# Three adaLN halves move from TensorE to VectorE, one of them into the S5-input stage, and the weight stream gets six buffers instead of seven

## The chip, the cores and the metric

One core of one Trainium2 chip. The metric is the device time of one launch, in microseconds, as the median of several runs; the profiled execution is one more launch, with its own time.

## What is computed

One conditioned decoder block on 256 tokens of width 2048, all in fp32. The condition vector `c` gives six vectors by one product with a 2048 x 12288 matrix (adaLN): shift, scale and gate for the mixer and for the MLP.

```
ada = (cond @ w_ada + b_ada)
sh1, sc1, gt1, sh2, sc2, gt2 = split(ada, 6)
u = rmsnorm(h, g_mix) * (1 + sc1) + sh1
q, kc, vc, ks_, vs_, kw, vw, g_nsa, u_ssm, g_merge = split(u @ w_in, ...)
y_a = nsa_attention(q, kc, vc, ks_, vs_, kw, vw, g_nsa, ...)
y_s = gelu(s5_ssm(u_ssm, ...))
y_b = y_s * sigmoid(y_s @ w_glu + b_glu)
g_a, g_b = split(sigmoid(g_merge), 2)
h = h + gt1 * ((g_a * y_a + g_b * y_b) @ w_out)
u2 = rmsnorm(h, g_mlp) * (1 + sc2) + sh2
h = h + gt2 * (square(relu(u2 @ w_up)) @ w_down)
return rmsnorm(h, g_final)
```

`sh1` and `sc1` are needed at once. `gt1`, `sh2`, `sc2` are needed behind the output projection, and `gt2` at the end: these are the later adaLN vectors.

## The kernel before

All weights flow through one stream of units. A unit loads one raw tile of 128 x 1024 fp32 values (512 KB) with one DMA on SyncE's queue (L210) into a ring of `RAW` = 7 buffers; the load of unit i+7 is issued at the start of turn i (i+5 while the generator `outs` is at work). A weight unit is split for an exact product: ScalarE copies it to `hi` in a shorter type (the helper at L117), VectorE computes `lo` = raw − hi (L120), and TensorE runs three matmuls for each 128 x 128 block, hi by hi, hi by lo and lo by hi (L315, L317, L318), two units behind the copy. An adaLN unit is not split: it takes the raw tile as it lies.

The list `units` is written in order of the stages: `sh1`/`sc1` with the first columns of `w_in`, the compressed keys and values (`vs`, 16 value tiles, and `compress`), the stage called E, gate A (`ga`), queries (`q`), gate B (`gb`), `glu`, `out`, `up`, `down`. E holds the last six value tiles and the tile of the attention gates; beside them the generator `in` makes the S5 inputs in 16 steps, each with 16 small matmuls (L809) and four ScalarE copies of 128 x 256 from PSUM. Generators like it (the S5 scan in gate A, q and the start of gate B, its outputs later in gate B, attention beside `glu`) are moved on by the count of weight units; adaLN units don't count.

The later vectors come in halves of 1024 columns, 16 raw tiles each. Six of them (`gt1`, `sh2`, `sc2`) are put between the weight units of E, gate A, q, gate B, `glu` and `out`; the table `ADA2` says how many tiles each of these stages takes, in this order, and `ADA_PE` which halves go over TensorE. There are two forms:

- on TensorE (`ada2_pe_units`): a pair of raw tiles is contracted with `cond` in 32 small matmuls (L998), four pairs fill a quarter, then ScalarE copies, transposes (L1007) and a VectorE reduction (L1009);
- on VectorE (`ada2_units`): 16 operations on 128 x 1024 add raw tile times `cond` column into an accumulator (L129, after one at L124), then four matmuls with ones (L965), a copy, four small transposes (L974), one addition.

Before the change `ADA2` gives E none and `glu` two halves; halves 0, 1, 3, 4, 5 go over TensorE, half 2 (in gate B) over VectorE. The two halves of `gt2`, in the up stage, are on VectorE in both kernels.

`weave(main, extra, tail=6, head=0)` spreads the extra units over the main ones up to the last `tail`:

```
    want = max(0, min(len(extra), (i + 1 - head) * len(extra) // (len(main) - tail - head)))
    res += extra[ie:want]
```

E calls it with seven main units and the default tail of six, so that all extra units come right behind the first main unit. `W_GLU` is (6, 10) and `W_OUT` is (8, 0), as (tail, head). In `out` each weight unit of the first 1024 columns also prepares its block of the mixed y, with turns between VectorE and ScalarE (L129 RX, L117 RB, L129 RB).

Of the kernel before, what the change touches and what calls it, by code (L numbers as in the profile page):

```python
# [9 lines left out]
FT = mybir.dt.float32  # L10
# [13 lines left out]
    0, 2048, 3072, 3584, 4096, 4608, 5120, 5168, 7216, 9264)  # L24
A_SH1, A_SC1, A_GT1, A_SH2, A_SC2, A_GT2 = (i * D for i in range(6))

RAW, HI, LO = 7, 3, 3
SPLIT = 2
ADA2 = [0, 16, 16, 16, 32, 16]
ADA_PE = (0, 1, 3, 4, 5)  # L30
SCAN_END = 0.4
ATTN_WAIT = 5
AS0, AS1 = 2, 13
# [48 lines left out]
def block_kernel(ctx, tc, cst_in, x, c, w_ada, b_ada, g_mix, w_in, w_ck2, pe_ck,  # L82
# [8 lines left out]
    sp = ctx.enter_context(tc.tile_pool(name="staging", bufs=1))  # L91
# [3 lines left out]
    def bank(tag):  # L95
        return pp_.tile([128, 512], FT, tag=tag, name=tag)
# [4 lines left out]
    def stage():  # L101
        return sp.tile([128, 512], FT, tag="st", name="st", bufs=ST)

    def big4():
        return sp.tile([128, 1024], FT, tag="s4", name="s4", bufs=2)

    def region(tag, n):
        return rp.tile([128, n], FT, tag=tag, name=tag)
# [7 lines left out]
    def copy(out, in_, scale=1.0):  # L116
        A.activation(out=out, in_=in_, func=AF.Copy, scale=scale)  # L117

    def tt(out, a, b, op):
        V.tensor_tensor(out=out, in0=a, in1=b, op=op)  # L120

    def ts(out, a, s1, op1, s2=None, op2=None):
        if s2 is None:
            V.tensor_scalar(out=out, in0=a, scalar1=s1, scalar2=None, op0=op1)  # L124
        else:
            V.tensor_scalar(out=out, in0=a, scalar1=s1, scalar2=s2, op0=op1, op1=op2)

    def stt(out, a, s, b, op0, op1):
        V.scalar_tensor_tensor(out=out, in0=a, scalar=s, in1=b, op0=op0, op1=op1)  # L129
# [59 lines left out]
    def defer(n, fn):  # L189
        later.setdefault(now[0] + n, []).append(fn)  # L190
# [220 lines left out]
    def merge(a, b, lead=LEAD, tail=TAIL):  # L411
        res = a[:lead]
        a = a[lead:]
        ia = 0
        for ib, u in enumerate(b):
            res.append(u)
            want = min(len(a), (ib + 1) * len(a) // (len(b) - tail))
            res += a[ia:want]
            ia = want
        return res  # L420
# [45 lines left out]
    def keep_x():  # L466
        nc.gpsimd.dma_start(out=d_xT, in_=xT)
        yield
# [480 lines left out]
    def ada2_units(vec, half, tag):  # L949
        off = (A_GT1, A_SH2, A_SC2, A_GT2)[vec] + 1024 * half  # L950
        hold = {}

        def run(u, kt):
            if kt == 0:
                hold["a"] = big4()
                ts(hold["a"], u.raw, cond[:, 0:1], OP.mult)
            else:
                stt(hold["a"], u.raw, cond[:, kt:kt + 1], hold["a"], OP.mult, OP.add)
            if kt == 15:
                defer(FIN_GAP, fin1)  # L960

        def fin1():
            ps = bank(tag)
            for i in range(2):
                PE.matmul(out=ps[32 * i:32 * i + 32, :], lhsT=ones32, rhs=hold["a"][:, 512 * i:512 * i + 512],  # L965
                          start=True, stop=True, tile_position=(0, 32 * i))
            hold["s"] = stage()
            copy(hold["s"][0:64], ps[0:64, :])
            defer(FIN_GAP, fin2)

        def fin2():
            ps = bank(tag)
            for j in range(4):
                PE.transpose(ps[:, 64 * j:64 * j + 64], hold["s"][0:64, 128 * j:128 * j + 128], ident[0:64, 0:64])  # L974
            k0 = 16 * vec + 8 * half
            bk = 32 + 16 * vec + 8 * half
            tt(ada2[:, k0:k0 + 8].rearrange("p (h j) -> p h j", h=2),
               ps[:, 0:256].rearrange("p (j h n) -> p h j n", j=4, h=2)[:, :, :, 0],
               bada_c[:, bk:bk + 8].rearrange("p (h j) -> p h j", h=2), OP.add)
            if vec == 2 and half == 1:  # L980
                stt(s2, sc2_c, 1.0, gmlp_c, OP.add, OP.mult)
        return [Unit([(lambda r: r, w_ada[0, kt * 128:(kt + 1) * 128, off:off + 1024])],
                     lambda u, k=kt: run(u, k), gemm=False) for kt in range(16)]
# [523 lines left out]
    with tc.manual_schedule():  # L1507
        units += ada1_units(0)
        for ci in range(1, len(chunks)):
            units += merge(ada1_units(ci), first_pass_units(ci - 1))  # L1510
        units += first_pass_units(len(chunks) - 1)
        e2 = []
        for h in range(6):
            if h in ADA_PE:
                e2 += ada2_pe_units(h // 2, 2 * (h % 2)) + ada2_pe_units(h // 2, 2 * (h % 2) + 1)
            else:
                e2 += ada2_units(h // 2, h % 2, "T12")
        marks["vs"] = len(units)
        vs = vs_units()
        units += vs[:VA] + weave(vs[VA:VB], compress_units(), 0) + vs[VB:VC]  # L1520
        marks["E"] = len(units)
        dist = iter(np.cumsum([0] + ADA2))

        def some(a=[next(dist)]):
            lo_, a[0] = a[0], next(dist)
            return e2[lo_:a[0]]
        units += weave(vs[VC:] + gate_unit(), some())
        marks["ga"] = len(units)
        units += weave(proj_units(C_GA, d_g, 0, AF.Tanh, 0.5, True), some())
        marks["q"] = len(units)  # L1530
        units += weave(proj_units(C_Q, d_q, 0, AF.Copy, HD ** -0.5, True), some())
        marks["gb"] = len(units)
        units += weave(proj_units(C_GB, d_g, 16, AF.Tanh, 0.5, False), some(), *W_GB)
        marks["glu"] = len(units)
        units += weave(glu_units(), some(), *W_GLU)
        marks["out"] = len(units)
        units += weave(out_units(), some(), *W_OUT)
        marks["up"] = len(units)
        up = up_units()
        up[0].lo_first = up[1].lo_first = True  # L1540
        units += up[:UP_WAIT] + weave(up[UP_WAIT:], [u for h in range(2) for u in ada2_units(3, h, "T3")])
        marks["down"] = len(units)
        units += down_units()

        xs, r2 = prelude()

        def at_(name, f, nxt):
            return int(marks[name] + f * (marks[nxt] - marks[name]))
        bgs = [
            dict(name="x", gen=x_chain(xs, r2), start=0, end=6, total=6, tick=True),  # L1550
            dict(name="xw", gen=keep_x(), start=marks["vs"] - KX, end=marks["vs"] - KX, total=1),
            dict(name="ld", gen=s5_loads(), start=LD0, end=LD0, total=1, tick=True),
            dict(name="ld2", gen=s5_loads2(), start=LD1, end=LD2, total=4, tick=True),
            dict(name="p1", gen=s5_prep(), start=P10, end=PB, total=P1A, tick=True),
            dict(name="p2", gen=s5_operands(), start=PB + 1, end=marks["vs"] - P11, total=P1N + 4 * sum(CY) + IDLE + IDLE2, tick=True),
            dict(name="cmp", gen=compress_setup(), start=marks["vs"] - 2, end=marks["vs"] + 3, total=12),
            dict(name="lam", gen=s5_lambda(), start=marks["vs"] + EM0, end=marks["vs"] + EM1, total=12, tick=True),
            dict(name="keep", gen=s5_keep(), start=marks["vs"] + EM1 + 1, end=marks["E"] - 2, total=4, tick=True),
            dict(name="chan", gen=s5_channels(), start=marks["vs"] + U0, end=marks["vs"] + U1, total=4, tick=True),
            dict(name="stk", gen=s5_inputs(), start=marks["vs"] + KI, end=marks["vs"] + KI, total=1),  # L1560
            dict(name="in", gen=(x_ for _ in range(1) for x_ in un["E"]), start=marks["E"] + 1, end=marks["ga"] - 1, total=16),
            dict(name="scan", gen=s5_scan(), start=marks["ga"], end=at_("gb", SCAN_END, "glu"), total=128),
            dict(name="mat0", gen=s5_matrices(0), start=marks["q"] + CL0, end=marks["q"] + CL1, total=4, tick=True),
            dict(name="mat1", gen=s5_matrices(1), start=marks["gb"] + CM0, end=marks["gb"] + CM1, total=4, tick=True),
            dict(name="outs", gen=s5_outputs(), start=at_("gb", SCAN_END, "glu") + 1, end=marks["glu"] - 1, total=17),
            dict(name="load", gen=attn_setup(), start=marks["glu"] + AS0, end=marks["glu"] + AS1, total=13),
            dict(name="tb", gen=load_tb(), start=marks["glu"] + TB0, end=marks["glu"] + TB1, total=4, tick=True),
            dict(name="attn", gen=attention(), start=marks["glu"] + ATTN_WAIT, end=marks["out"] - 2, total=34),
        ]
        run_units(bgs)  # L1570
# [47 lines left out]
```

## Time and profile before

| | us |
|---|---|
| median of 3 runs | 1780.44 |
| lowest, highest | 1776.47, 1782.63 |
| the profiled execution, its time | 1776.92 |
| its span | 1775.1 |
| TensorE busy | 1718.9 (97%) |
| TensorE weight loads busy | 1620.6 (91%) |
| VectorE busy | 1108.5 (62%) |
| ScalarE busy | 856.3 (48%) |

The mean granted TensorE clock of the span is 0.989. The stages lie in the span like this: first stage to about 290, `vs` and `compress` to 329, E to 381, gate A and q to about 565, gate B to 701, `glu` and attention to 895, `out` to 1010, up to 1376, down to the end. TensorE's busy time is an upper measure, since its matmuls overlap; a window of the trace gives for each engine its busy time, the count of its instructions, the granted clock and the share of the DMA engines.

### The profile page before, as it was taken

The page shows a single profiled execution, that of the slowest core. Times are in us where ns is not written, and L with a number is a line of the kernel's source. Part 1 is how long each engine was busy: PE and PEld are TensorE (multiplying, and loading weights), DVE is VectorE, ACT ScalarE, POOL GpSimd, SP SyncE. Part 2 cuts the span into 40 slices and gives each one's busy share as a digit, 9 for nine tenths or more (in the row PEclk, how much of TensorE's full clock was granted, in tenths as well). Part 3 has the DMA queues.
Part 4 walks back from the last instruction along what each step waited for, and adds up shares of the span by engine and source line. Part 5 has one row for each costly group of instructions (what it writes and reads, how often), then busy time and mean ns, then how long its engine had stood idle before and what let it go on. Part 6 is the DMA issues. An engine that isn't in the chain of part 4 may idle for free.

```text
span 1775.1 us, 37647 instructions
## 1 busy us (share of the span) xinstructions
PE 1718.9 (97%) x15710; PEld 1620.6 (91%) x15710; DVE 1108.5 (62%) x2032; ACT 856.3 (48%) x1379; POOL 29.4 (2%) x51
## 2 busy tenths in 40 slices
PE   6999999999999999999999999999999999999997
PEld 4788898789999988888899999999999999999997
DVE  4868468347888966666656575555555555565554
ACT  3433443754333477655544454444444544464444
POOL 1000000300000000000000000000000000000000
PEclk8999999999999999999999999999999999999998
DMA  9988756858888867876667567777777565556662
GB/s 349 327 275 315 260 180 206 267 160 296 274 274 283 254 211 243 296 244 211 214 198 262 176 219 235 235 227 224 240 234 227 179 183 184 181 176 184 184 181 81
DMA packets 121802, 406.26 MB, mean 229 GB/s; under 512 B 13904, under 2 KB 18480, under 8 KB 120864
## 3 DMA queue, kind: packets, MB, share of 16 engines
q1 hardware_dynamic: 114480, 385.49, 67.1%
q10 hardware_dynamic: 5408, 9.75, 1.5%
q0 software_dynamic: 1744, 8.62, 1.4%
q8 instruction: 123, 2.02, 0.4%
q14 instruction: 47, 0.39, 0.1%
HBM read 384.84 MB, written 16.88 MB: 226 GB/s over the span
## 4 chain that ended last, share of the span: by engine, by line
PE 87%; DVE 5%; ACT 4%; DMA 2%; issue 1%; ACTq 0%; SPq 0%; DVEq 0%
PE A L315 25%; PE A L317 24%; PE A L318 24%; PE T L998 2%; DVE lo L120 2%; PE T L343 2%; ACT hi L117 1%; ACT RX L117 1%; DMA raw<-in_l_ada_dram 1%; PE T L809 1%; PE A L897 1%; DMA raw<-in_l_vals_dram 1%; PE A L899 1%; PE A L898 1%; PE T L737 0%
## 5 line engine op out<-in xcount | busy, mean ns | idle before, releaser
L120 DVE TENSOR_TENSOR lo<-raw,hi 128x1024 fp32r<-128x1024 f32 (+1 forms) x497 | 607.0, 1223 | 507.8 <-ACT hi L117 504.0
L117 ACT ACTIVATE hi<-raw 128x1024 fp32r<-128x1024 f32 (+1 forms) x497 | 523.1, 1055 | 580.5 <-PE A L317 539.0
L315 PE MATMUL A<-RU,hi 128*128 128x256 f32 x2560 | 740.2, 289 | 3.3 <-ACT hi L117 1.5
L318 PE MATMUL A<-RU,lo 128*128 128x256 f32 x2560 | 728.0, 284 | 1.5 <-DVE lo L120 1.5
L317 PE MATMUL A<-RU,hi 128*128 128x256 f32 x2560 | 727.8, 284 | 0.0
L315 PEld LDWEIGHTS A<-RU,hi 128*128 128x128 f32 x2560 | 494.3, 193 | 27.7 <-issue 20.9
L318 PEld LDWEIGHTS A<-RU,lo 128*128 128x128 f32 x2560 | 494.4, 193 | 2.0 <-DVE lo L120 1.9
L317 PEld LDWEIGHTS A<-RU,hi 128*128 128x128 f32 x2560 | 494.7, 193 | 0.3 <-DVE RU L129 0.2
L315 PE MATMUL A<-RB,hi 128*128 128x256 f32 x1280 | 363.9, 284 | 1.4 <-ACT RB L117 1.2
L317 PE MATMUL A<-RB,hi 128*128 128x256 f32 x1280 | 362.6, 283 | 0.2
L318 PE MATMUL A<-RB,lo 128*128 128x256 f32 x1280 | 362.2, 283 | 0.0
L315 PEld LDWEIGHTS A<-RB,hi 128*128 128x128 f32 x1280 | 245.7, 192 | 3.4 <-ACT RB L117 1.6
L317 PEld LDWEIGHTS A<-RB,hi 128*128 128x128 f32 x1280 | 245.7, 192 | 0.6 <-DVE RB L129 0.5
L318 PEld LDWEIGHTS A<-RB,lo 128*128 128x128 f32 x1280 | 245.6, 192 | 0.0
L117 ACT ACTIVATE RB<-RX 128x256 fp32r<-128x256 f32 x160 | 64.3, 403 | 27.4 <-DVE RX L129 27.4
L120 DVE TENSOR_TENSOR RX<-A,RX 128x512 f32<-128x512 f32 x60 | 40.4, 687 | 30.2 <-PE A L318 29.2
L129 DVE SCALAR_TENSOR_TENSOR s<-raw,cond,s 128x1024 f32<-128x1024 f32 x45 | 57.6, 1279 | 0.1
L117 ACT ACTIVATE RX<-T 128x256 f32<-128x256 f32 (+2 forms) x81 | 39.8, 638 | 35.8 <-PE T L1204 26.6
L120 DVE TENSOR_TENSOR RB<-RX,RB 128x256 fp32r<-128x256 f32 x128 | 53.4, 418 | 1.6 <-ACT RB L117 1.6
L343 PE MATMUL T<-raw,cond 128*32 128x256 f32 x512 | 40.8, 413 | 10.0 <-DMA raw<-in_l_ada_dram 10.0
L998 PE MATMUL T<-raw,cond 128*32 128x128 f32 x1280 | 43.2, 276 | 2.0 <-ACT RX L117 2.0
L998 PEld LDWEIGHTS T<-raw,cond 128*32 128x32 f32 x1280 | 32.5, 109 | 8.4 <-ACT RX L117 4.2
(237 smaller groups left out, 1248.1 us busy)
## 6 DMA issues: line engine op xcount, KB each, us to landing
raw<-in_l_ada_dram SPq DMA_DIRECT2D x144, 512.0 KB, 4.9
raw<-in_w_in_dram SPq DMA_DIRECT2D x144, 512.0 KB, 4.6
raw<-in_w_up_dram SPq DMA_DIRECT2D x128, 512.0 KB, 4.2
raw<-in_w_down_dram SPq DMA_DIRECT2D x128, 512.0 KB, 4.5
raw<-in_w_ada_dram SPq DMA_DIRECT2D x48, 512.0 KB, 4.1
raw<-in_w_glu_dram SPq DMA_DIRECT2D x32, 512.0 KB, 5.1
raw<-in_w_out_dram SPq DMA_DIRECT2D x32, 512.0 KB, 5.8
raw<-in_l_keys_dram SPq DMA_DIRECT2D x16, 512.0 KB, 4.4
```

The lines of the kernel that those rows point to most:

```text
L117: A.activation(out=out, in_=in_, func=AF.Copy, scale=scale)
L120: V.tensor_tensor(out=out, in0=a, in1=b, op=op)
L129: V.scalar_tensor_tensor(out=out, in0=a, scalar=s, in1=b, op0=op0, op1=op1)
L315: PE.matmul(out=o, lhsT=w.hi[:, at], rhs=xh, start=first and j % 2 == 0, stop=False, skip_group_check=True)
L317: PE.matmul(out=o, lhsT=w.hi[:, at], rhs=xl, start=False, stop=False, skip_group_check=True)
L318: PE.matmul(out=o, lhsT=w.lo[:, at], rhs=xh, start=False, stop=last, skip_group_check=True)
L343: PE.matmul(out=ps[q:q + 32, :], lhsT=cond[:, t0 + t:t0 + t + 1].to_broadcast([128, 32]), rhs=r[:, t, :], start=t0 == 0, stop=t0 == 12, ti ...
L809: PE.matmul(out=ps[h][:, (w * 2 + r_) * 128:(w * 2 + r_) * 128 + 128], lhsT=bl[c4 // 2][64 * h:64 * h + 64, (gw + w) % 16, r_, :], rhs=stk ...
L897: PE.matmul(out=o, lhsT=xh, rhs=u.hi[:, at], start=kt == 0, stop=False)
L898: PE.matmul(out=o, lhsT=xl, rhs=u.hi[:, at], start=False, stop=False)
L899: PE.matmul(out=o, lhsT=xh, rhs=lo[:, at], start=False, stop=kt == 15)
L998: PE.matmul(out=ps[q:q + 32, 0:128], lhsT=cond[:, kt:kt + 1].to_broadcast([128, 32]), rhs=r[:, kt % 8, :], start=kt < 4, stop=kt >= 12, ti ...
```

## The change

The ring of raw tiles has six buffers. `ADA2` gives each of the six stages one half. Only halves 1 (gate A) and 2 (q) go over TensorE; halves 0 (E), 3 (gate B), 4 (`glu`) and 5 (`out`) go over VectorE. The accumulators have three buffers instead of two, and the halves 4 and 5 use the PSUM bank T3 for their ending.

```diff
-RAW, HI, LO = 7, 3, 3
+RAW, HI, LO = 6, 3, 3
-ADA2 = [0, 16, 16, 16, 32, 16]
-ADA_PE = (0, 1, 3, 4, 5)
+ADA2 = [16, 16, 16, 16, 16, 16]
+ADA_PE = (1, 2)
...
-        return sp.tile([128, 1024], FT, tag="s4", name="s4", bufs=2)
+        return sp.tile([128, 1024], FT, tag="s4", name="s4", bufs=3)
...
-                e2 += ada2_units(h // 2, h % 2, "T12")
+                e2 += ada2_units(h // 2, h % 2, "T12" if h < 4 else "T3")
```

SyncE's queue around the start of E (the value tiles `l_vals`, the adaLN tiles `w_ada`, the gate tile `l_gate`, and a store of compress, `d_c`):

```order
 L210 DMA raw<-in_l_vals_dram 128x1024 x2
 L760 DMA d_c<-RX 128x1024
-L210 DMA raw<-in_l_vals_dram 128x1024 x2
+L210 DMA raw<-in_l_vals_dram 128x1024
+L210 DMA raw<-in_w_ada_dram 128x1024
 L760 DMA d_c<-RX 128x1024
-L210 DMA raw<-in_l_vals_dram 128x1024 x3
+L210 DMA raw<-in_w_ada_dram 128x1024 x15
+L210 DMA raw<-in_l_vals_dram 128x1024 x5
 L210 DMA raw<-in_l_gate_dram 128x768
```

All 16 adaLN loads now stand ahead of the last five value tiles.

VectorE beside attention, from the end of one head's scores to the next weight tile's lo, before:

```order
L1169 TENSOR_REDUCE RX<-T_9198 128x1
L1170 TENSOR_REDUCE RX<-T_9198 128x2
L124 TENSOR_SCALAR RX<-RX 128x3
L120 TENSOR_TENSOR lo<-raw,hi 128x1024
L120 TENSOR_TENSOR RX<-RX,cst 128x2x16
L1187 TENSOR_REDUCE RX<-RX 128x2
```

and of the changed kernel:

```order
L1169 TENSOR_REDUCE RX<-T_9217 128x1
L1170 TENSOR_REDUCE RX<-T_9217 128x2
L124 TENSOR_SCALAR RX<-RX 128x3
L129 SCALAR_TENSOR_TENSOR s_9099<-raw,cond,s_9099 128x1024
L120 TENSOR_TENSOR lo<-raw,hi 128x1024
L120 TENSOR_TENSOR RX<-RX,cst 128x2x16
```

One accumulation (`s`) has come in ahead of the lo; it is so once for each of 16 weight tiles.

VectorE in the first half of `out`, two weight tiles with their mixing, before:

```order
L120 TENSOR_TENSOR lo<-raw,hi 128x1024
L129 SCALAR_TENSOR_TENSOR RX<-RB_8555,RX 128x256
L129 SCALAR_TENSOR_TENSOR RB_10742<-RX,RB_10742 128x256
L120 TENSOR_TENSOR lo<-raw,hi 128x1024
L129 SCALAR_TENSOR_TENSOR RX<-RB_8555,RX 128x256
L129 SCALAR_TENSOR_TENSOR RB_10742<-RX,RB_10742 128x256
```

and of the changed kernel, three tiles:

```order
L120 TENSOR_TENSOR lo<-raw,hi 128x1024
L129 SCALAR_TENSOR_TENSOR RX<-RB_8613,RX 128x256
L129 SCALAR_TENSOR_TENSOR RB_10476<-RX,RB_10476 128x256
L129 SCALAR_TENSOR_TENSOR s_10525<-raw,cond,s_10525 128x1024
L120 TENSOR_TENSOR lo<-raw,hi 128x1024
L129 SCALAR_TENSOR_TENSOR RX<-RB_8613,RX 128x256
L129 SCALAR_TENSOR_TENSOR RB_10476<-RX,RB_10476 128x256
L120 TENSOR_TENSOR lo<-raw,hi 128x1024
```

An accumulation stands behind two of three tiles there.

## Rows read from the trace of the kernel before

**Rows 1.** The page: busy time and share of each engine, and the shares by engine of the chain that ended last.

```profile
PE 1718.9 (97%) x15710; PEld 1620.6 (91%) x15710; DVE 1108.5 (62%) x2032; ACT 856.3 (48%) x1379; POOL 29.4 (2%) x51
...
PE 87%; DVE 5%; ACT 4%; DMA 2%; issue 1%; ACTq 0%; SPq 0%; DVEq 0%
```

**Rows 2.** Windows by stage: E, gate A and q with the start of gate B, attention, `out`. Columns: the window, its length, busy time (and instructions) of TensorE, its weight loads, VectorE, ScalarE, GpSimd, the granted TensorE clock, the DMA share, GB/s.

```profile
329.00:381.00 52.00, 46.26 (x400) 38.48 (x400) 12.43 (x17) 40.66 (x79) 9.25 (x17) 1.00 0.61 190
381.00:637.00 256.00, 255.62 (x2471) 250.21 (x2472) 214.03 (x592) 98.77 (x118) 0.00 (x0) 0.99 0.81 267
...
756.00:868.00 112.00, 108.75 (x1128) 91.72 (x1127) 69.26 (x220) 59.36 (x191) 0.00 (x0) 1.00 0.66 222
868.00:1010.00 142.00, 140.03 (x1305) 132.78 (x1297) 90.04 (x168) 68.91 (x128) 0.56 (x1) 1.00 0.69 230
```

**Rows 3.** The page's costliest groups: busy time, mean ns of one, idle time before.

```profile
L129 DVE SCALAR_TENSOR_TENSOR s<-raw,cond,s 128x1024 f32<-128x1024 f32 x45 | 57.6, 1279 | 0.1
```

**Rows 4.** Timeline of TensorE in gate A (a pair of adaLN tiles and the weight tiles around it) and in gate B (the ending of the half on VectorE). Columns: start, length, engine, line, operation, count.

```profile
389.07 1.08 PE L998 MATMUL T<-raw,cond 128*32 128x128 f32 x32
390.08 0.38 PE L315 MATMUL A<-RU,hi 128*128 128x256 f32 x1
...
398.89 1.08 PE L998 MATMUL T<-raw,cond 128*32 128x128 f32 x32
...
701.65 1.05 PE L965 MATMUL T<-s,cst 128*32 128x512 f32 x4
702.63 0.39 PE L315 MATMUL A<-RU,hi 128*128 128x256 f32 x1
```

**Rows 5.** Timeline of ScalarE in E: three steps of the S5 inputs (12 copies), the hi copy of value tile 13, and the first of gate A. The last column is the idle time before, with what ended it.

```profile
335.77 5.50 ACT L117 ACTIVATE RX<-T 128x256 f32<-128x256 f32 x12 [2.99 <-DMA raw<-in_l_vals_dram]
341.06 1.06 ACT L117 ACTIVATE hi<-raw 128x1024 fp32r<-128x1024 f32 x1
...
373.19 1.06 ACT L117 ACTIVATE hi<-raw 128x1024 fp32r<-128x1024 f32 x1
```

**Rows 6.** Timeline of VectorE in E: the lo of value tile 11, then of 12 and 13.

```profile
331.07 1.23 DVE L120 TENSOR_TENSOR lo<-raw,hi 128x1024 fp32r<-128x1024 f32 x1 [2.55 <-ACT hi L117]
332.81 1.23 DVE L120 TENSOR_TENSOR lo<-raw,hi 128x1024 fp32r<-128x1024 f32 x1 [0.51 <-ACT hi L117]
342.16 1.23 DVE L120 TENSOR_TENSOR lo<-raw,hi 128x1024 fp32r<-128x1024 f32 x1 [8.13 <-ACT hi L117]
```

**Rows 7.** Windows of 5 us, columns as in Rows 2: the start of E, the start of gate A, and a stretch of the first stage.

```profile
325.00:330.00 5.00, 5.00 (x28) 4.07 (x27) 2.75 (x5) 2.31 (x4) 3.59 (x7) 1.00 1.04 343
335.00:340.00 5.00, 4.32 (x51) 3.69 (x48) 0.00 (x0) 4.23 (x10) 0.00 (x0) 1.00 1.03 411
...
380.00:385.00 5.00, 3.62 (x22) 3.57 (x23) 4.90 (x14) 1.33 (x2) 0.00 (x0) 0.78 0.61 204
...
75.00:80.00 5.00, 1.30 (x20) 0.36 (x16) 4.93 (x9) 0.00 (x0) 0.00 (x0) 0.90 1.00 361
80.00:85.00 5.00, 5.00 (x41) 4.07 (x34) 4.34 (x15) 1.06 (x1) 0.00 (x0) 0.76 1.03 411
```

**Rows 8.** The view of the adaLN tiles of the VectorE form (`w_ada`): time from issue to landing.

```profile
DMA to landing us min/median/max: 3.5/4.1/5.8
```

**Rows 9.** Timeline of TensorE at the start of gate A.

```profile
381.38 0.32 PE L922 MATMUL T<-cst,st 48*128 48x48 f32 x2 [2.52 <-ACT st L917]
381.63 0.39 PE L315 MATMUL A<-RU,hi 128*128 128x256 f32 x1
```

**Rows 10.** Timeline beside attention: TensorE at the start of two heads that lie three weight tiles apart, then VectorE through these three tiles.

```profile
760.40 0.62 PE L1153 MATMUL T<-RX 128*128 128x272 f32 x2
782.63 0.62 PE L1153 MATMUL T<-RX 128*128 128x272 f32 x2
...
776.62 0.18 DVE L120 TENSOR_TENSOR RX<-RX,cst 128x32 f32<-128x32 f32 x1
...
778.51 0.42 DVE L129 SCALAR_TENSOR_TENSOR RX<-RB,A 128x256 f32<-128x256 f32 x1
...
783.29 0.45 DVE L120 TENSOR_TENSOR T<-T,cst 128x272 f32<-128x272 f32 x1
...
789.10 0.41 DVE L129 SCALAR_TENSOR_TENSOR RX<-RB,A 128x256 f32<-128x256 f32 x1
...
792.23 0.45 DVE L120 TENSOR_TENSOR T<-T,cst 128x272 f32<-128x272 f32 x1 [0.81 <-PE T L1153]
797.70 1.23 DVE L120 TENSOR_TENSOR lo<-raw,hi 128x1024 fp32r<-128x1024 f32 x1 [2.91 <-ACT hi L117]
```

**Rows 11.** Timeline in the first half of `out`: VectorE from lo to lo, then TensorE at two pairs that lie three weight tiles apart.

```profile
917.26 1.23 DVE L120 TENSOR_TENSOR lo<-raw,hi 128x1024 fp32r<-128x1024 f32 x1 [0.52 <-ACT hi L117]
...
919.30 0.42 DVE L129 SCALAR_TENSOR_TENSOR RB<-RX,RB 128x256 fp32r<-128x256 f32 x1 [0.48 <-ACT RB L117]
920.25 1.23 DVE L120 TENSOR_TENSOR lo<-raw,hi 128x1024 fp32r<-128x1024 f32 x1 [0.52 <-ACT hi L117]
...
919.74 1.08 PE L998 MATMUL T<-raw,cond 128*32 128x128 f32 x32
929.57 1.08 PE L998 MATMUL T<-raw,cond 128*32 128x128 f32 x32
```

**Rows 12.** Waits of 20 to 330 (waiting instruction, what released it: idle us, times, longest), and the page's DMA issues (KB, median us to landing).

```profile
PE T L343 <- DMA raw<-in_l_ada_dram: 3.7, 2, 3.1
...
raw<-in_w_down_dram SPq DMA_DIRECT2D x128, 512.0 KB, 4.5
```

## Prediction

> **What bounds the kernel now.** I read three things, in this order. First the page's busy shares and the chain that ended last: TensorE works 1718.9 us of the 1775.1 us span and holds 87% of that chain [rows 1], so in the mean every TensorE microsecond removed is a microsecond gained. Second, because that mean covers stages with different limits, the windows by stage [rows 2]. The gate-A stage (381 to 637) is TensorE alone, 255.62 of 256. The stage with the S5 inputs (329 to 381, called E below) is not: TensorE 46.26 of 52, VectorE nearly idle with 12.43, ScalarE busy for 40.66. Attention (756 to 868) has TensorE at 108.75 of 112 and VectorE at 69.26; the output projection (868 to 1010) 140.03 of 142 beside 90.04. Third, in E, attention and the output projection, the rows of the engines that feed TensorE, since there the question is whether something else ends later once TensorE has less to do. "Half" below is one 1024-column piece of an adaLN vector, 16 raw tiles.
>
> **What TensorE gives up.** Three halves leave it: two beside GLU and attention, one beside the output projection; the gate-A stage and the q stage carry one each, as before. A half is 8 pairs of raw tiles; a pair stands on TensorE from 389.07 to 390.08, 1.01 us, and between two pairs lie three weight tiles: 389.07 to 398.89 is 9.82, so a weight tile costs (9.82−1.01)/3 = 2.94 [rows 4]. The half is 8.1, three are 24.2. Each of the three halves on VectorE still needs the four matmuls with ones, 701.65 to 702.63, 0.98 [rows 4]; the small transposes of the old form and of the new one I set against each other. Net −21.3, if TensorE paced every place where something goes in or out. On VectorE a half is 16 operations of 1.28 us [rows 3], 20.5 us; whether they are hidden decides everything, stage by stage.
>
> **E: +13, bounds +4 and +19.** This is the one stage that receives work without losing any. The 16 raw tiles all stand right behind the eleventh of the 16 value tiles, and ScalarE runs in program order. So the hi copy of value tile 12 stands in ScalarE's queue ahead of the 13 S5-input steps that remain (of 16; 3 run before it), each four copies, 5.50/3 = 1.83 us [rows 5]; that copy waits for its tile, whose load stands behind 16 adaLN loads in a ring of six. VectorE is free once the lo of value tile 11 is done, 331.07+1.23 = 332.3 [rows 6]. The load of value tile 12 needs the buffer of the 11th adaLN tile: 332.3 + 11×1.28 + some 1.5 for late arrivals (the DMA queues are full here, share 1.04 at 325 to 330 and 1.03 at 335 to 340 [rows 7]) = 347.9. An adaLN tile lands 4.1 us after its issue [rows 8], and value tiles come the same way: the hi copy starts near 352.
>
> From the hi copy at 341.06 (value tile 13) to the first of gate A at 373.19 the stage today takes 32.1 us for five weight tiles and 13 steps [rows 5]; from value tile 12 there are six tiles, 1.06 us of ScalarE more: 33.2. Gate A then starts at 385.2 instead of 373.19: +12. Meanwhile TensorE finishes the tiles and the steps that it has and idles some ten microseconds. What that does to the clock the trace shows twice. It granted 0.76 in 80 to 85 after TensorE had been busy for 1.30 of the 5 us before, and 0.78 in 380 to 385 [rows 7], around an idle of 2.52 us; behind that, 48 matmuls took 381.63 to 389.07, 7.44 us, instead of the 5.88 of two weight tiles [rows 9, 4]. I add 1 (the steps that follow are bound by ScalarE). The Trainium skill ("TensorE: Matmul & The Clock Gate", section "HAM oscillation — how this bites in real kernels") says that idle gaps between bursts of matmuls put the array back to its low clock, a rule that speaks against this change; the rows of the clock agree with it.
>
> Low bound: the block starts at 329 and nothing arrives late: 329 + 11×1.28 + 3.5, the shortest landing [rows 8], = 346.6; then ScalarE without a gap, 13×1.83 + 6×1.06 = 30.2, to 376.8: +3.6. High bound: the 16 tiles come at the 343 GB/s of 325 to 330 [rows 7], 24.5 us for 8.4 MB, 4.0 more than the accumulation and 2.5 more than I allowed; landing at 5.8 instead of 4.1; 2 more of clock: +19.
>
> **GLU and attention: −6.5, bounds −15 and +1.** Today three weight tiles with two heads and three pairs take 22.23 us, 760.40 to 782.63 [rows 10]. Without the pairs TensorE needs 22.23 − 3×1.01 = 19.20. In the changed order every weight tile has one accumulation on VectorE, in front of its lo. A tile's turn on VectorE is lo, head work, accumulation. For the first of two heads: 1.23, then 783.29 to 789.51 = 6.22, then 1.28: 8.73. For the second: 1.23, then 792.23 to the next lo at 797.70 = 5.47, in which the accumulation fits (the lo waits 2.91 for the hi copy, which stands behind the exponentials on ScalarE): 6.70. For the tile between: 1.23, 776.62 to 778.93 = 2.31, 1.28: 4.82 [rows 10]. The sum, 20.25, is above 19.20: VectorE, in turn with ScalarE, becomes the limit, and the gain is 2.0 of 3.0. Over 16 tiles that is −10.6 at best. Part is lost, because the ring assumes that ScalarE answers as fast as now though its inputs come later: I take −7.5, two thirds of it, and add 0.98 for the ones-matmuls. Bounds: all 16 pairs gained, −16.2 + 0.98; none, +1.
>
> **Output projection: +1, bounds −7 and +5.** In its first half each weight tile needs four operations in turn between VectorE (y mixing) and ScalarE; from lo to lo they take 917.26 to 920.25, 2.99 us, with VectorE idle 0.48 and 0.52 in it [rows 11]. TensorE with its pairs takes (929.57−919.74)/3 = 3.28 a tile [rows 11] and is just the slower. The change takes the 0.34 off and puts an accumulation behind two of three tiles: of its 1.28 the 0.52 are free, 0.76 are not. The mean turn is 2.99 + 0.76×2/3 = 3.50, so VectorE takes over: 0.22 a tile, over some 12 tiles (the first four were prepared ahead) +2.6. In the second half there is no mixing and TensorE paces: 2.7 pairs less, −2.7; the ones-matmuls +0.98. Low: all eight pairs gained, −8.1 + 0.98. High: all 16 tiles at +0.22, no gain in the second half.
>
> **Six weight buffers: +1.5, bounds 0 and +6.** With TensorE pacing, a tile asked for about four tiles ahead of its use has 4×2.94 = 11.8 us for a landing of 4.5 [rows 12]: free in gate A, q, up and down. In the first stage TensorE does wait for raw tiles, 3.7 us in two waits [rows 12], the DMA share is 1.00 to 1.03 at 75 to 85 [rows 7], and one buffer less lets the queue run dry once or twice sooner; and while the scan's outputs are made the kernel loads two fewer ahead, now four. One wait like those (1.85) is the price that I round down to 1.5; 0 if queued DMA hides it, 6 if each wait comes three times. The third accumulator buffer and the other PSUM bank for the last two halves add no instruction; they cost nothing while no half waits for another, which the order of the stages keeps apart.
>
> **Sum.** +13 − 6.5 + 0.9 + 1.5 = +8.9 on 1776.92 of the profiled execution: 1785.8. The median of the runs is 1780.44, 3.5 above it; on the median the forecast is 1789.
>
> **Rivals**, on the median:
> - *TensorE paces everywhere and E is cheap.* −21.3 + 3.6 = 1763. For it: 97% busy [rows 1]. Against it: E at 46.26 of 52 [rows 2] and the two rings above. The Trainium skill ("Perfetto Trace Analysis", section "Identifying the Most-Contended Engine") tells to optimise the engine of highest occupancy first, and to judge TensorE by its weight loads (91% here); by that alone the time would be 1759. Chance 0.05.
> - *Faster: the rings close.* It happens if VectorE's three turns beside attention come in under 19.20, as they may where operations overlap waits that I count twice, and under 2.94 in the output projection. E still +13: 13 − 15.2 − 7.1 + 1.5 = −7.8, 1773. Chance 0.13.
> - *E's block is hidden, the rest as forecast.* 3.6 − 6.5 + 0.9 + 1.5 = −0.5: 1780. For it: VectorE is free there. Against it: value tile 12 stands behind 11 accumulations in any case. Chance 0.20.
> - *Forecast*, 1784 to 1795, 1789 the middle. Chance 0.52.
> - *Worse:* E at +19 and the ring of six at +6: 19 − 6.5 + 0.9 + 6 = 19.4, 1800. Chance 0.10.
>
> **Numbers.** 0.3% is 5.3 us, about what a measurement of this kernel can tell from no change: 1775.1 to 1785.8. Faster: the first rival and most of the second, 0.17. Same: the third, the second's edge and the forecast's low end, 0.25. Slower 0.58. The range 1774 to 1799 leaves out the first, about half of the second and of the last, 0.17.
>
> **What would show it.** In E: VectorE's 16 accumulations in one block from about 332, the hi copy of value tile 12 near 352, TensorE idle about ten microseconds before it with a granted clock below 0.9, the first gate-A hi copy near 385. Beside attention: three tiles in 20.2 to 21.5 us instead of 22.23, lo waiting less for hi. In the output projection: turns of 2.99 and 3.75. In gate A, q, up and down: the same lengths as before. It is wrong if the hi copy comes by 347, if three tiles beside attention take 19, or if gate A shows waits for raw tiles.

## The result and the profile after

The changed kernel takes 1795.89 us (median; 1795.19 to 1796.13), the kernel before 1780.49 beside it: ratio 1.0091, 95% interval 1.0074 to 1.0107. It is slower, by 15.4 us, where 8.6 had been forecast. The profiled execution took 1795.87, 18.95 above that of before.

The page of the profile after, against [rows 1]:

```profile
PE 1707.7 (95%) x14942; PEld 1605.2 (89%) x14942; DVE 1162.1 (65%) x2071; ACT 853.9 (48%) x1358; POOL 29.3 (2%) x51
...
PE 76%; DVE 12%; ACT 6%; DMA 4%; issue 2%; ACTq 0%; SPq 0%; DVEq 0%
...
L129 DVE SCALAR_TENSOR_TENSOR s<-raw,cond,s 128x1024 f32<-128x1024 f32 x90 | 115.1, 1279 | 6.8 <-DMA raw<-in_w_ada_dram 6.3
```

TensorE lost 11.2 us of busy time and 11 points of the chain that ended last; VectorE, ScalarE and DMA took them. VectorE has three times 15 more accumulations at the same 1279 ns.

Every weight tile has one hi copy on ScalarE, and both kernels have 497 of them in the same order. The time of the same copy in both traces, subtracted, shows where the difference arises:

| hi copy of | before | after | later by | change in the stretch |
|---|---|---|---|---|
| 25th weight tile, first stage | 137.41 | 141.24 | 3.8 | +3.8 |
| third value tile | 293.19 | 297.18 | 4.0 | +0.2 |
| tenth tile of gate A (E lies between) | 405.83 | 432.55 | 26.7 | +22.7 |
| last of gate B | 699.57 | 727.23 | 27.7 | +1.0 |
| GLU, where attention begins | 746.63 | 774.57 | 27.9 | +0.3 |
| GLU, 18 tiles on | 876.98 | 892.68 | 15.7 | −12.2 |
| first of the output projection | 898.54 | 916.13 | 17.6 | +1.9 |
| its 17th, end of the first half | 953.97 | 974.25 | 20.3 | +2.7 |
| first of up | 1003.78 | 1022.40 | 18.6 | −1.7 |
| last of down | 1752.56 | 1771.21 | 18.6 | 0.0 |

Gate A, q, up and down run at the same pace in both. E alone is more than the whole loss. Its rows on VectorE, against [rows 6], and ScalarE, against [rows 5] (start, length, engine, line, operation, idle time before with what ended it):

```profile
336.60 1.23 DVE L120 TENSOR_TENSOR lo<-raw,hi 128x1024 fp32r<-128x1024 f32 x1 [2.57 <-ACT hi L117]
337.88 0.75 DVE L124 TENSOR_SCALAR s<-raw,cond 128x1024 f32<-128x1024 f32 x1
342.01 14.49 DVE L129 SCALAR_TENSOR_TENSOR s<-raw,cond,s 128x1024 f32<-128x1024 f32 x11 [3.38 <-DMA raw<-in_w_ada_dram]
357.38 1.28 DVE L129 SCALAR_TENSOR_TENSOR s<-raw,cond,s 128x1024 f32<-128x1024 f32 x1 [0.88 <-DMA raw<-in_w_ada_dram]
360.33 1.28 DVE L129 SCALAR_TENSOR_TENSOR s<-raw,cond,s 128x1024 f32<-128x1024 f32 x1 [1.66 <-DMA raw<-in_w_ada_dram]
362.04 2.60 DVE L129 SCALAR_TENSOR_TENSOR s<-raw,cond,s 128x1024 f32<-128x1024 f32 x2 [0.43 <-DMA raw<-in_w_ada_dram]
```

```profile
364.52 1.06 ACT L117 ACTIVATE hi<-raw 128x1024 fp32r<-128x1024 f32 x1 [17.42 <-DMA raw<-in_l_vals_dram]
365.49 3.60 ACT L117 ACTIVATE RX<-T 128x256 f32<-128x256 f32 x8
...
399.89 1.07 ACT L117 ACTIVATE hi<-raw 128x1024 fp32r<-128x1024 f32 x1
```

The block of 16 stands in VectorE's order where it was expected (from 337.88 on), but every pause in it, 3.38, 0.88, 1.66 and 0.43, ends with a tile's landing, and so does ScalarE's wait of 17.42 us for value tile 12. DMA shows why: landing times of the adaLN tiles from 320 to 400, against the 4.1 of [rows 8], and windows of 5 us with the columns of [rows 7]:

```profile
DMA to landing us min/median/max: 6.1/9.2/13.8
```

```profile
345.00:350.00 5.00, 5.00 (x34) 3.85 (x33) 4.86 (x5) 2.11 (x5) 0.00 (x0) 0.82 1.03 411
350.00:355.00 5.00, 3.98 (x32) 3.01 (x28) 4.89 (x4) 0.00 (x0) 3.93 (x8) 1.00 1.03 379
355.00:360.00 5.00, 0.00 (x0) 0.00 (x0) 2.75 (x3) 0.00 (x0) 0.43 (x1) 0.70 1.05 293
360.00:365.00 5.00, 0.00 (x0) 0.00 (x0) 3.85 (x3) 0.47 (x1) 0.00 (x0) 0.50 1.02 379
365.00:370.00 5.00, 1.92 (x4) 0.19 (x4) 1.25 (x2) 5.00 (x11) 0.06 (x1) 0.50 0.99 372
```

The DMA share stays near one through the whole block. TensorE stands still for 13.45 us, from 353.98 to 367.43, and its clock falls to the lower level, 0.50:

```profile
367.43 1.92 PE L965 MATMUL T<-s,cst 128*32 128x512 f32 x4 [13.45 <-ACT RX L117]
```

### The profile page after: what moved, and what is told of

It is laid out like the page before. It is cut to its first block, busy times and chain, and to the rows that moved or that the text cites. A ratio compares the mean times of both kernels' runs of the same rounds, so it can differ in the third digit from the quotient of the medians.

```text
span 1794.1 us, 36164 instructions
## 1 busy us (share of the span) xinstructions
PE 1707.7 (95%) x14942; PEld 1605.2 (89%) x14942; DVE 1162.1 (65%) x2071; ACT 853.9 (48%) x1358; POOL 29.3 (2%) x51
## 4 chain that ended last, share of the span: by engine, by line
PE 76%; DVE 12%; ACT 6%; DMA 4%; issue 2%; ACTq 0%; SPq 0%; DVEq 0%
PE A L315 23%; PE A L317 23%; PE A L318 22%; DVE lo L120 4%; ACT hi L117 2%; DMA raw<-in_l_ada_dram 2%; DVE s L129 2%; PE T L343 1%; DVE RX L120 1%; DVE RX L124 1%; PE T L998 1%; DMA raw<-in_w_ada_dram 1%; ACT RX L1178 1%; ACT RX L117 1%; DVE T L120 1%
## 5 line engine op out<-in xcount | busy, mean ns | idle before, releaser
L129 DVE SCALAR_TENSOR_TENSOR s<-raw,cond,s 128x1024 f32<-128x1024 f32 x90 | 115.1, 1279 | 6.8 <-DMA raw<-in_w_ada_dram 6.3
L343 PE MATMUL T<-raw,cond 128*32 128x256 f32 x512 | 42.4, 421 | 12.3 <-DMA raw<-in_l_ada_dram 12.3
L117 ACT ACTIVATE RX<-T 128x256 f32<-128x256 f32 (+2 forms) x81 | 40.0, 635 | 20.9 <-PE T L1204 9.4
L120 DVE TENSOR_TENSOR RX<-t,t 128x128 f32<-128x128 f32 x127 | 37.1, 292 | 4.4
L120 DVE TENSOR_TENSOR t<-RX,l2r 128x128 f32<-128x128 f32 x127 | 36.5, 287 | 1.6
```

The source lines that it names most:

```text
L343: PE.matmul(out=ps[q:q + 32, :], lhsT=cond[:, t0 + t:t0 + t + 1].to_broadcast([128, 32]), rhs=r[:, t, :], start=t0 == 0, stop=t0 == 12, ti ...
```

## Experiments

The kernel before was timed again beside each set of runs. Its medians were 1780.49 beside the changed kernel, 1777.82 (the half in E over TensorE, E spread, E without a half, six buffers the first time), 1778.18 (three accumulators the first time, and the last two experiments) and 1779.03 (half the bytes, and the second pair of six buffers and three accumulators). A ratio is to the kernel before of its own set; a plain difference from the changed kernel holds up to 2.7 us of the difference between these medians.

**The half in E over TensorE.** Same loads at the same place, no accumulation on VectorE.

```diff
-ADA_PE = (1, 2)
+ADA_PE = (0, 1, 2)
```

> The changed kernel with the half in E contracted on TensorE instead of VectorE; the 16 loads stand where they stood. Theory A (DMA sets the pace of the block): the hi copy of value tile 12 comes at 360 to 365 as in the changed kernel, since the tiles land no faster, and the time is within 3 us of it. Theory B (VectorE's 16 accumulations set the pace, as in my sum): a tile's buffer is free as soon as it has landed, and the hi copy comes some 8 us sooner, 1788.

Measured: 1796.17 us, ratio to before 1.0102 (1.0086 to 1.0117). The hi copy of value tile 12:

```profile
361.76 0.28 ACT L117 ACTIVATE s<-T 128x128 f32<-128x128 f32 x1 [2.33 <-PE T L998]
364.26 0.28 ACT L117 ACTIVATE s<-T 128x128 f32<-128x128 f32 x1 [2.22 <-PE T L998]
364.80 1.06 ACT L117 ACTIVATE hi<-raw 128x1024 fp32r<-128x1024 f32 x1 [0.26 <-DMA raw<-in_l_vals_dram]
```

It comes at 364.80 against 364.52, but not because the queue was full all the way. TensorE reaches its first pair only at 345.98, behind S5-input steps that wait for ScalarE, where VectorE began at 337.88. Until then no buffer is given back, and the queue runs empty; windows of 5 us with the columns of [rows 7]:

```profile
345.98 1.93 PE L998 MATMUL T<-raw,cond 128*32 128x128 f32 x32 [1.56 <-ACT RX L117]
```

```profile
345.00:350.00 5.00, 3.62 (x64) 2.77 (x64) 0.00 (x0) 1.20 (x4) 0.00 (x0) 0.50 0.35 112
355.00:360.00 5.00, 2.55 (x72) 1.67 (x76) 0.07 (x1) 0.56 (x2) 0.00 (x0) 1.00 1.02 405
```

From 355 on the share is above one again, and the last four pairs are ready 2.5 to 3.0 us apart, 1.25 to 1.5 a tile, without VectorE: that is the pace of theory A. That the two hi copies agree within 0.3 us is in part chance, and the time of this run alone does not decide between the theories.

**Half the bytes in E.** Each of the 16 tiles loads its first 512 columns alone and VectorE works through them twice; the other half of its columns is left out.

```diff
-        return [Unit([(lambda r: r, w_ada[0, kt * 128:(kt + 1) * 128, off:off + 1024])],
+        return [Unit([(lambda r: r[:, 0:n], w_ada[0, kt * 128:(kt + 1) * 128, off:off + n])],
...
+            for c in range(0, 1024, n):
+                o, i_ = hold["a"][:, c:c + n], u.raw[:, 0:n]
```

> The changed kernel with half the bytes in E: each of the 16 adaLN tiles there loads only its first 512 columns, and VectorE accumulates these twice (two operations of 512 columns in place of one of 1024), so that VectorE's work stays what it was; left out is the second half of that half's columns, and the vector gt1 is not right. Theory A (the queue of 16 full loads sets the time): the tiles land at twice the pace, VectorE's 20 to 22 us become the limit, and the hi copy of value tile 12 comes at 355 to 358 instead of 364.5, about where my forecast of 352 lies once the 4 us of the first stage are added; the time is 6 to 9 us less, 1787 to 1790. Theory B (the accumulations set it): 364 again, 1795.

Measured: 1790.76 us (1.0069, 1.0053 to 1.0084), 5.1 less than the changed kernel, or 3.7 when each is taken against the kernel before beside it. The profiled execution is the slowest of the four, 1795.15, only 0.7 below that of the changed kernel; E costs 20.4 in it instead of 22.7. Its VectorE and ScalarE:

```profile
338.44 1.23 DVE L120 TENSOR_TENSOR lo<-raw,hi 128x1024 fp32r<-128x1024 f32 x1 [3.08 <-ACT hi L117]
...
342.50 18.64 DVE L129 SCALAR_TENSOR_TENSOR s<-raw,cond,s 128x512 f32<-128x512 f32 x28 [0.39 <-DMA raw<-in_w_ada_dram]
...
360.75 1.06 ACT L117 ACTIVATE hi<-raw 128x1024 fp32r<-128x1024 f32 x1 [12.51 <-DMA raw<-in_l_vals_dram]
```

The half tiles land in 3.7 us in the median, and 28 of the operations run without a pause on VectorE. From the lo of value tile 11 to the hi copy of tile 12 it takes 22.3 us, against 27.9 in the changed kernel (336.60 to 364.52) and 20.9 in my sum (331.07 to 352). So with the queue relieved the forecast step is nearly met. Of the 5.6 us between the two kernels 2.5 lie ahead of the issue of value tile 12 and 3.1 in its landing, 6.2 instead of 9.3. That the copy came at 360.75 and not at 355 to 358 is 5.2 us of first stage instead of 4, 2.2 at tile 11, and the 1.4 left. The expected gain of 6 to 9 was too large, because VectorE's 21 us stand right behind the DMA limit: each of the two needs about 1.3 us a tile, and relieving one does not free E.

**E's tiles spread** over its seven weight units.

```diff
-        units += weave(vs[VC:] + gate_unit(), some())
+        units += weave(vs[VC:] + gate_unit(), some(), 0)
```

> The changed kernel with the 16 adaLN tiles of E spread over its seven weight units (two or three behind each) instead of all behind the first. Theory A (the block costs because 16 loads in a row fill the DMA queues, so that the next value tile lands late and the S5-input steps stand behind its hi copy): the steps go on between, E costs 3 to 8 instead of 22.8, 1776 to 1781. Theory B (16 accumulations and 8.4 MB more are too much for this stage wherever they stand): E still costs over 15, 1788 or more.

Measured: 1780.96 us (1.0022, 1.0013 to 1.0031), 3.1 more than the 1777.82 of before beside it and 14.9 less than the changed kernel, or 12.3 when each is taken against the kernel before beside it. E from 342 to 392:

```profile
342.00:392.00 50.00, 44.63 (x360) 36.64 (x360) 29.22 (x31) 40.02 (x77) 8.70 (x16) 0.93 0.93 309
```

The same accumulations, 16 of them, and the same bytes, in a stage whose DMA share is 0.93 over 50 us instead of 1.03 in one lump. E costs 6.9 there (4.5 late ahead of it, 11.5 behind it). The block's place, not its work, is what the other 16 us were: theory A. Loads and accumulations are spread together here, so the run does not tell them apart; and to leave the block in one lump but put the S5-input steps ahead of that hi copy was not tried.

**E without a half**; gate A carries two, on TensorE.

```diff
-ADA2 = [16, 16, 16, 16, 16, 16]
-ADA_PE = (1, 2)
+ADA2 = [0, 32, 16, 16, 16, 16]
+ADA_PE = (0, 1, 2)
```

> The changed kernel without the half in the S5-input stage E: it goes back to gate A and over TensorE, gate A then carries two halves (32 tiles). Theory A (the stage E alone costs 22.8 us, as the shift from weight tile to weight tile shows): -22.8 and +8.9 for one more half on TensorE, about -14, so 1782. Theory B (E costs the 13 that I forecast and the rest of the shift is a late start that any load pattern gives): -13 + 8.9, about -4, 1792.

Measured: 1783.5 us (1.0029, 1.0019 to 1.0038), 12.4 less, or 9.7 when each is taken against the kernel before beside it: nearer to theory A's 14 than to the 4 of theory B. In its trace E costs 0.8, which is theory A; gate A grows by 12 instead of the 8.9 that TensorE's pairs take. What the other 3 are was not followed further.

**Six buffers alone, and six buffers with three accumulators**, both on the kernel before; run twice each.

```diff
-RAW, HI, LO = 7, 3, 3
+RAW, HI, LO = 6, 3, 3
```

> The kernel before with six weight buffers and nothing else. Theory A (the ring of six is what delays the first stage): the first stage ends 3.9 us later as in the changed kernel, the end of gate B some 1 us later, everything else is the same: +4 to +6, about 1785. Theory B (my prediction's term): +1.5, within what can't be told from before, and the 3.9 us of the changed kernel come from somewhere else.

and with, in addition,

```diff
-        return sp.tile([128, 1024], FT, tag="s4", name="s4", bufs=2)
+        return sp.tile([128, 1024], FT, tag="s4", name="s4", bufs=3)
```

> The kernel before with six weight buffers and three accumulator buffers, nothing else: no half is moved. Theory A (the third buffer lets GpSimd's second memset go some 44 us sooner, since it no longer waits for the buffer of t4; the 2 MB store of x that stands behind it in GpSimd's queue goes out at 111 instead of 154, right behind the other 2 MB store, and the key tiles land late): the first stage ends 3 to 4 us later than in the kernel before, GpSimd's store is issued near 112, and the total is +4, about 1782. Theory B (the late key tiles of the changed kernel come from the ring of six, at another phase): as with six buffers alone, +0.5 to +1.5, and the first stage as there.

Six buffers alone: 1780.55 (1.0015, 1.0005 to 1.0024), with the first stage 0.7 us later in the profile: theory B. With the third accumulator buffer: 1781.08 (1.0008, 0.9995 to 1.0022). GpSimd of the first kernel and then of the second:

```profile
109.28 0.97 POOL L698 MEMSET s<- 128x1024 f32 x1
154.15 0.95 POOL L698 MEMSET s<- 128x1024 f32 x1 [43.90 <-DVE RX L120]
155.04 0.54 POOL L467 DMA_DIRECT2D d_xT<-RX  x1
```

```profile
111.82 1.86 POOL L698 MEMSET s<- 128x1024 f32 x2
113.61 0.54 POOL L467 DMA_DIRECT2D d_xT<-RX  x1
```

The order of GpSimd's queue is the same in both, but its second memset needs a buffer of the accumulators' pool. With two buffers it waits 43.9 us until VectorE has done with the first tile of that pool (`t4` in the kernel), and with it waits the store of x, 2 MB, behind it. With three the store goes out at once, 2.3 us behind another 2 MB store of the same queue, and the key tiles that are loaded then land later. Issued between 95 and 130, they need 6.0 us in the first kernel and 11.9 in the second:

```profile
raw<-in_l_keys_dram SPq DMA_DIRECT2D x4, 512.0 KB, 6.0
```

```profile
raw<-in_l_keys_dram SPq DMA_DIRECT2D x4, 512.0 KB, 11.9
```

The early store and the late tiles of theory A are there. Whether this costs the whole kernel anything was the point of the second pair:

> The kernel before with six weight buffers, beside the next one on the same chip. Theory A (the store of x sent out 44 us sooner costs 3 us in the first stage, in every execution): 3 us less than the next one, and in its profile weight tile 24 at 137 to 139.5. Theory B (that delay comes and goes between executions, whatever the accumulators' buffers): no difference of the two medians.

> The kernel before with six weight buffers and three accumulator buffers. Theory A: 3 us more than the one before, and weight tile 24 at 140.5 to 141.5 in its profile. Theory B: the same median.

Measured: 1779.36 (1.0009, 1.0000 to 1.0017) and 1781.58 (1.0011, 1.0002 to 1.0020); the medians differ by 2.2, the means by 0.7. In the profiles the 25th weight tile comes 0.7 and 1.8 us later than before with six buffers, 3.3 and 3.6 later with three accumulators; the changed kernel, E spread, E over TensorE, half the bytes and E without a half, all with three, have 3.2 to 4.8, and the two kernels below, with two, 1.1 and 2.0. But the times of the 21 runs of either kernel differ by 0.6 in the mean, with a standard error of 0.6. So what the profiled executions show, some 2 us at this tile and 4.5 at the last one, all the runs together do not bear out. The early store is shown; a loss of time by it is not, and stays open. Six buffers alone cost 0.9 to 1.5 parts in a thousand, 1.6 to 2.7 us.

**E spread, the accumulator of E with a buffer of its own, a late ending of the half beside GLU.**

```diff
-        return sp.tile([128, 1024], FT, tag="s4", name="s4", bufs=3)
+        return sp.tile([128, 1024], FT, tag="s4", name="s4", bufs=2)
...
+                hold["a"] = sp.tile([128, 1024], FT, tag="acc", name="acc", bufs=1) if own else big4()
...
-                defer(FIN_GAP, fin1)
+                defer(gap, fin1)
...
-                e2 += ada2_units(h // 2, h % 2, "T12" if h < 4 else "T3")
+                e2 += ada2_units(h // 2, h % 2, "T12" if h < 4 else "T3", h == 0, 12 if h == 4 else FIN_GAP)
```

> The kernel with E's tiles spread, with three edits that lie in different stages: the accumulator of E has a buffer of its own while the other accumulators have two again; the ending of the half beside GLU is put off by ten units, behind attention. Theory A: GpSimd's second memset waits again, the store of x goes out near 154 and the first stage gains 3 to 4 us on the kernel with E spread; the step of 1.9 us at the end of GLU (the heads' transposes wait for the PSUM bank of that ending) is gone. Together -5, about 1776. Theory B (neither a store nor a bank is behind these steps): 1781 as before the edits.

Measured: 1779.49 us (1.0006, 0.9994 to 1.0019); by the two ratios this is 2.8 us better than E spread without the edits, by the medians 1.8, not 5, and the two intervals overlap. The store goes out at 155.45, and the 25th tile is 1.1 late instead of 4.1; but E costs 9.8 instead of 6.9. In the changed kernel the first transposes behind it stood 1.3 us, until VectorE's addition had read the bank:

```profile
PE T L1203 <- DVE ada L120: 1.3, 1, 1.3
```

With the late ending this wait is gone, but the step between the same two tiles is 1.4 instead of 1.9: from 874 to 890 the granted clock is 0.89, after TensorE had stood 2.5 us for ScalarE's scaling of a head's probabilities (L1195). So the bank's wait is shown, and that taking it away gains something is not.

**A recombination from the kernel before.** Six buffers, E empty, the three halves of gate A and q woven tile by tile with one of them on VectorE, one VectorE half beside GLU, the half of the output projection back on TensorE.

```diff
+ADA2 = [0, 24, 24, 16, 16, 16]
+ADA_PE = (0, 2, 5)
...
+        q0, q1, q2 = e2[:16], e2[16:32], e2[32:48]
+        e2 = [u for k in range(16) for u in (q0 + q2)[2 * k:2 * k + 2] + [q1[k]]] + e2[48:]
```

> Built from the kernel before: six weight buffers; E carries no half; the three halves of gate A and q are woven tile by tile, one of them on VectorE with a buffer of its own, two on TensorE; gate B one on VectorE; GLU one on VectorE with a late ending; the output projection one on TensorE. If VectorE's free 42 us in gate A and q take 16 accumulations (20.5 us) beside TensorE's pace, these stages grow by 0 to 5 us and GLU gives back 12 to 14: 1766 to 1771, faster than both kernels. If the scan on VectorE is delayed by them, gate A and q grow by 10 or more and nothing is left of it, 1777 or more.

Measured: 1775.68 us over 11 runs, before 1778.18; ratio 0.9983, interval 0.9970 to 0.9995. It is the fastest of all, though by less than expected: gate A and q grow by 3.5 us, within the bounds, gate B by 1.4, GLU with its end gives back 10.9, and the first stage is 2.4 late.

## Why the prediction was right and where it was wrong

The direction and the range held (1795.89 in 1774 to 1799); the size was off by 7. By its own steps, on the profiled executions:

- **E, +13: measured +22.7, outside its bounds.** The order of events was right: a block on VectorE, the hi copy of value tile 12 behind it, the steps behind that, TensorE idle, the clock low. The step that failed is the price of a transfer. I took 4.1 us for a landing, which [rows 8] show for adaLN tiles in gate B and the up stage, where the DMA share is 0.65 to 0.83, and 1.5 us for all late arrivals, though [rows 7] already had the share above 1. The load of value tile 12, its time to landing, and that of the five adaLN loads issued from 343.3 to 348.6:

```profile
355.21 0.33 SPq L210 DMA_DIRECT2D raw<-in_l_vals_dram  x1
...
DMA to landing us min/median/max: 9.3/9.3/9.3
...
DMA to landing us min/median/max: 6.1/6.2/6.3
```

  Value tile 12 was expected at 352 and came at 364.5. Of the 12.5 us between, 4.0 are the first stage, 1.5 were there at tile 11 already (336.60 against 331.07 + 4.0), 1.8 are pauses in the block beyond the 1.5 allowed (the load went out at 355.21 instead of 347.9), and 5.2 are the landing, 9.3 instead of 4.1. With the queue full in a steady run a load landed in 6.2; the other 3 us came with the slower rate behind 350, of which the last section tells. From the hi copy to gate A 35.4 us passed instead of 33.2, with the granted clock at 0.50 until 370: 2.2 where I had put 1 for the clock (not separated further). My high bound did contain the rate of 343 GB/s, but with it a landing of 5.8.
- **GLU and attention, −6.5: measured −12.2, then +1.9 at its end, −10.3.** The rows of three tiles beside attention:

```profile
802.70 1.22 DVE L120 TENSOR_TENSOR lo<-raw,hi 128x1024 fp32r<-128x1024 f32 x1 [1.01 <-ACT hi L117]
...
807.25 1.21 DVE L120 TENSOR_TENSOR lo<-raw,hi 128x1024 fp32r<-128x1024 f32 x1
...
815.15 1.22 DVE L120 TENSOR_TENSOR lo<-raw,hi 128x1024 fp32r<-128x1024 f32 x1
...
821.03 1.23 DVE L120 TENSOR_TENSOR lo<-raw,hi 128x1024 fp32r<-128x1024 f32 x1 [1.01 <-ACT hi L117]
```

  The three turns are 4.55, 7.90 and 5.88, in the sum 18.33, against 4.82, 8.73 and 6.70 in mine. Head work on VectorE is shorter in them (808.39 to 813.95, 5.56 instead of 6.22): the 6.22 held waits on the other engines; which of the removed instructions shortened them was not separated. But these three are among the shortest. The start of the fifth and of the fifteenth head on TensorE after, and of the fifteenth before ([rows 10] have the fifth, 760.40):

```profile
784.36 0.62 PE L1153 MATMUL T<-RX 128*128 128x272 f32 x2
...
883.68 0.62 PE L1153 MATMUL T<-RX 128*128 128x272 f32 x2
...
871.55 0.62 PE L1153 MATMUL T<-RX 128*128 128x272 f32 x2
```

  Ten heads took 99.32 us after and 111.15 before, so two heads with their three tiles took 19.86 instead of 22.23 in the mean. That lies between the 19.20 that I took for TensorE and my 20.25: the ring was right to 0.4, and the second rival, which needs less than 19.20, is met by single stretches and not by the stage. A gain of 2.37 in three tiles is 12.6 over 16, near the 12.2 measured. The term that was mis-sized is the cut from −10.6 to −7.5 for a ScalarE that answers later, which no row supported. TensorE no longer paces alone, being busy 98.86 of 108 us (784 to 892) beside VectorE's 92.47. The +1.9 at the end I had not seen.
- **Output projection, +0.9: measured +2.7 and −1.7, +1.0.** Right in both halves (+2.6 and −1.7 in the sum), though from other levels: from lo to lo the twelve tiles took 3.15 each before (917.26 to 955.04) and 3.38 after (934.75 to 975.32), where I had 3.28, which is TensorE's pace, and 3.50. The turns were 3.58, 3.58 and 2.98. An accumulation takes the wait ahead of the next lo, as forecast, but adds 0.59 and not 0.76, since an operation that follows at once starts before the record of the one ahead ends (937.13 is 0.09 before 936.79 + 0.43, and 938.33 is 0.08 before 937.13 + 1.28):

```profile
934.75 1.22 DVE L120 TENSOR_TENSOR lo<-raw,hi 128x1024 fp32r<-128x1024 f32 x1 [0.53 <-ACT hi L117]
...
936.79 0.43 DVE L129 SCALAR_TENSOR_TENSOR RB<-RX,RB 128x256 fp32r<-128x256 f32 x1 [0.48 <-ACT RB L117]
937.13 1.28 DVE L129 SCALAR_TENSOR_TENSOR s<-raw,cond,s 128x1024 f32<-128x1024 f32 x1
938.33 1.22 DVE L120 TENSOR_TENSOR lo<-raw,hi 128x1024 fp32r<-128x1024 f32 x1
...
941.91 1.22 DVE L120 TENSOR_TENSOR lo<-raw,hi 128x1024 fp32r<-128x1024 f32 x1
...
944.89 1.23 DVE L120 TENSOR_TENSOR lo<-raw,hi 128x1024 fp32r<-128x1024 f32 x1 [0.52 <-ACT hi L117]
```

- **Six buffers, +1.5: the stretches meant by it measured +4.0 (first stage) and +1.3 (end of gate B).** Alone they cost about what I put, 1.6 to 2.7. In the profiled executions the larger loss in the first stage stands only in kernels with the third accumulator buffer, which I had costed at nothing: it adds no instruction, but the wait that it spares had been holding back a 2 MB store. All runs together show no loss by it that stands clear of the noise (0.6 ± 0.6 us), so where the rest of the 4.0 comes from stays open, and the 1.3 at the end of gate B was not traced.
- **Profiled execution to median.** I added the 3.5 us by which the median of before lies above its profiled execution. The changed kernel has its median at its profiled time, so this step was wrong by 3.5 and hid as much of the error. The 1780.44 came from three runs; beside the experiments the same kernel had medians of 1777.82 to 1779.03.

The sum of the parts is 22.7 − 10.3 + 1.0 + 5.2 = 18.6, the shift of the last weight tile. Against the forecast of 8.9, E and the six buffers were 9.7 and 3.7 too low and GLU 3.8 too high, so that half of the loss was not forecast. That the range held is in part luck: without the 3.5 us of the last step it would have ended at 1795.5, just below the 1795.87 of the profiled execution.

TensorE had no matmul from 353.98 to 367.43; its granted clock was 0.70 in 355 to 360, 0.50 in 360 to 370 and 0.59 in 370 to 375, and 1.00 only behind that, with the steps going on. The rule on idle gaps and the clock in the Trainium skill ("TensorE: Matmul & The Clock Gate", section "HAM oscillation — how this bites in real kernels"), cited in the prediction, agrees with these rows. The rule of the Trainium skill on the most-contended engine ("Perfetto Trace Analysis", section "Identifying the Most-Contended Engine"), by which TensorE's 91% would have given my 1759, did not hold for this change as a whole; beside attention, where TensorE had been the limit, 10.3 of the 15.2 us that it could give up were collected.

## What to carry to other kernels

Cost a moved load by the landing time of a stretch with as many loads in flight as it will have there, not by that of a stretch with a short queue, and spread a batch over the stage that hides it: the same 16 tiles cost 23 us in a lump and 7 when woven. When a pool gets one more buffer, list what its waits were holding back, on every queue, before calling it free. In a ring of two engines, take the mean over many turns: three turns were 18.33 here where the mean was 19.86, and waits inside a turn shrink when work moves.

## What was not expected of the hardware

With five or six loads of 512 KB in flight the queues moved 379 to 411 GB/s between 345 and 355 at a share of 1.03, which is 1.28 to 1.38 us a tile, by chance just what VectorE's accumulation takes; the time from issue to landing of the 16 was 6.1 to 13.8 us, and 6.2 in the steady run from 343 to 349. From 355 to 360 the rate was 293 with the share at 1.05. While eight of GpSimd's transfers of the S5 inputs ran (64 KB each, issued from 350.73 on), SyncE's loads took 3.36 us of all 16 engines per MB from 355 to 362 (80.1% of 7 us for 1.67 MB), against 2.60 from 345 to 355 (100.8% of 10 us for 3.88 MB). What slows the loads' own packets there was not tried; from 355.21 on the loads issued are also value tiles and no longer adaLN tiles.
